# Attention scores four units at a time, the second product over 64 rows in pairs

## The chip, the cores and the metric

The kernel runs on one core of a Trainium2 chip. The core has a matrix engine (TensorE, PE in the profile; its weight loads are the row PEld), three engines for elementwise work (VectorE or DVE, ScalarE or ACT, GpSimd or POOL) and SyncE (SP), whose queue issues most DMA transfers. Matrix products are written to PSUM, eight banks of 128 partitions by 512 floats. The metric is the time of one execution on the device in microseconds; the time before is 445.89 us, the median of three runs (445.73 to 446.54).

## The reference

One encoder layer on a sequence of 1024 tokens with 1024 features. Cut to what matters:

```
h = x @ W_in                                  # q_a,k_a,v_a,z_a, q_b,k_b,v_b,z_b
# group A, 8 heads of 64: 2-D neighbourhood attention on a 16 x 64 grid of tokens
s = q . k over the query's window (8 x 16) / 8 + rel_bias
y_a = softmax(s) @ v
# group B, 8 query heads, 2 key heads: rotary q and k, window |i - j| <= 128, a sink logit
s = q . k / 8, masked;  p = softmax([s, sink])[:-1];  y_b = p @ v
y = concat(y_a * silu(z_a), y_b * silu(z_b)) @ W_out
x = layer_norm(2**0.25 * x + y)
```

All inputs are float32. The kernel works with float16 products and keeps the accuracy by splitting a number into a high and a low half: a product is high x high + high x low + low x high.

## The kernel before, in words

The work has four stages: values (v) for all tokens (TensorE lines L630 and L684, up to about 60 us), six of the 21 other projections of 128 columns each (function `project`, L407), a loop of 128 attention steps (about 122 to 358 us), and the output projection with the layer norm (`out_mms`, L1145, and `final`).

A *unit* is one block of 128 queries of one head. Units 0 to 63 are group B ('b': head pair p, head j of the pair, block of 128 queries i, up to 384 keys); 64 to 127 are group A ('a': a block of 8 x 16 queries, b its column block and `half` its row half, with a window of 11 or 12 grid rows by 24 or 32 columns, 264 to 384 keys). In step i the loop does, among other things:

- `stage_qk` of unit i: two products into one PSUM bank of the tag "s" (L933 and L934), then one VectorE instruction (L943) that adds the bias or mask, takes the minimum and writes the negated scores to one of two tiles `sn`.
- `stage_exp` of unit i: ScalarE (L959) writes the exponentials back into the unit's PSUM bank.
- `stage_tr` of unit i-1: ScalarE (L969) and VectorE (L970) split the exponentials into high and low halves; a DMA transposes them. L970 is the last reader of the bank.
- every fourth step `stage_pv`: the products with the values of a *quad* of four units (L998, bank tag "t"), a step later `stage_on` (L1004, L1007) divides by the sums, and after every second quad `stage_ot` transposes (L1018, tag "t") and multiplies with the gate (L1021 for 'b', L1027 for 'a').
- the other 15 projections and the first part of the output projection as *filling*: `pump_to(u)` issues so many of their products that they are spread evenly over the steps, as the table FILL_AT says.

The queries of a head lie as a stack of 128 rows: for head j = 0 the high half in rows 0 to 63 and the low half in rows 64 to 127, for j = 1 the other way about. The high halves of the keys, `kh`, and the low halves, `kl`, are copied into both halves of the rows (L321 on GpSimd), so a product over 128 rows gives (q_high + q_low) times kh, and the next one (q_high + q_low) times kl:

```python
nc.tensor.matmul(ps[:, :m], q, sl[0], start=True, stop=False)
nc.tensor.matmul(ps[:, :m], q, sl[1], start=False, stop=True)
```

Each engine works off its instructions in the order in which the program writes them. TensorE, VectorE, ScalarE and GpSimd get the filling's evacuations and the splits of weights in between from small queues (`enq`, `pop`), a few per step. PSUM's eight banks are 2 of the tag "pj" (projections), 4 "s" and 2 "t"; a bank is given out again in turn and its next writer waits for its last reader. `m_scale` works out a common scale `zg`, `msc`, `zcol` for the gates in steps 2 to 9, on VectorE.

## Time and profile before

| | |
|---|---|
| median of three runs | 445.89 us |
| the profiled execution | 445.78 us |
| its span, first to last instruction | 444.0 us |
| mean granted TensorE clock | 0.997 |
| TensorE busy (products) | 437.4 us, 99% of the span |
| VectorE / ScalarE / GpSimd busy | 345.6 / 308.2 / 232.2 us |
| score products L933 and L934 | 128 + 128, 4.1% of the chain each |

How to read it: a row of a group gives line, engine, operation, output <- inputs, partitions x elements and type, the count, then busy time in us, the mean in ns of one instruction, and the idle time of the engine just before them with what ended it. A row of the timeline gives the start in us from the beginning of the span, the duration, engine, line, operation and count. Products overlap in the pipe, so the recorded time of one is longer than the distance to the next. The chain of waits is followed back from the last instruction, at each step to what released it.

### The profile page before, as it was taken

What the parts mean: (1) busy time and instruction counts of PE and PEld (TensorE: products, weight loads), DVE (VectorE), ACT (ScalarE), POOL (GpSimd) and SP (SyncE); (2) the same over time, 40 slices, a digit from 0 to 9 for tenths busy, and PEclk for the clock granted to TensorE, in tenths of its full rate; (3) what the DMA queues carried; (4) which work ended last, traced back from release to release, by engine and by line L of the source; (5) the groups of instructions that cost most, each with busy time, mean ns of one, the idle gap of its engine ahead of it and who ended that gap; (6) DMA issues with size and microseconds to landing.
All of it is one profiled execution on the core that took longest, in us unless ns stands there. A gap on an engine that the chain in (4) does not pass through costs nothing.

```text
span 444.0 us, 9533 instructions
## 1 busy us (share of the span) xinstructions
PE 437.4 (99%) x3275; PEld 252.9 (57%) x3275; DVE 345.6 (78%) x861; ACT 308.2 (69%) x717; POOL 232.2 (52%) x242
## 2 busy tenths in 40 slices
PE   9999999999999999999999999999999999999994
PEld 9987754444445565555555656555555654444442
DVE  5999938839989797776898888897767747179954
ACT  7798269866688998798978978797886876002211
POOL 1206834555837658868507638666762455005740
PEclk9999999999999999999999999999999999999998
DMA  8991178976849699687789998999999888101721
GB/s 298 316 362 62 28 249 257 311 264 251 300 98 177 131 190 159 135 149 150 153 165 171 202 173 184 208 180 225 197 201 235 149 198 316 49 0 71 257 76 71
DMA packets 133984, 81.76 MB, mean 184 GB/s; under 512 B 101296, under 2 KB 113328, under 8 KB 133680
## 3 DMA queue, kind: packets, MB, share of 16 engines
q1 hardware_dynamic: 133504, 80.67, 74.4%
q8 instruction: 25, 0.41, 0.4%
q10 hardware_dynamic: 432, 0.49, 0.3%
q14 instruction: 23, 0.19, 0.2%
HBM read 50.73 MB, written 9.96 MB: 137 GB/s over the span
## 4 chain that ended last, share of the span: by engine, by line
PE 92%; DMA 2%; DVE 2%; SPq 1%; ACT 1%; issue 0%; ACTq 0%
PE ps_pj L407 49%; PE ps_s L1145 9%; PE ps_t L998 7%; PE ps_pj L1145 5%; PE ps_t L1145 5%; PE ps_s L933 4%; PE ps_s L934 4%; PE ps_s L684 4%; PE ps_t L1018 2%; PE ps_pj L684 1%; PE ps_t L684 1%; DMA wr<-in_wt 1%; DMA xraw<-in_xT 1%; SPq L625 1%; DVE xm L498 1%; ACT x L455 0%
## 5 line engine op out<-in xcount | busy, mean ns | idle before, releaser
L407 PE MATMUL ps_pj<-xf,wh 128*128 128x512 f16 x672 | 202.6, 379 | 0.0
L407 PE MATMUL ps_pj<-xf,wl 128*128 128x512 f16 x336 | 127.3, 379 | 0.0
L407 PEld LDWEIGHTS <-wh 128*128 128x128 f16 x672 | 63.9, 98 | 60.1 <-issue 0.2
L959 ACT ACTIVATE ps_s<-sn,nm 128x385 f32<-128x385 f32 (+3 forms) x128 | 70.0, 547 | 29.6 <-DVE nm L943 28.6
L970 DVE SCALAR_TENSOR_TENSOR split<-ps_s,split 128x384 f16<-128x384 f32 (+2 forms) x128 | 65.5, 512 | 17.1 <-ACT split L969 16.2
L1145 PEld LDWEIGHTS <-m 128*128 128x128 f16 x408 | 38.8, 98 | 42.7
L969 ACT ACTIVATE split<-ps_s 128x384 f16<-128x384 f32 (+2 forms) x128 | 57.5, 449 | 2.4
L407 PEld LDWEIGHTS <-wl 128*128 128x128 f16 x336 | 32.9, 98 | 36.7
L943 DVE CUSTOM_DVE_ANT_0 sn<-ps_s,bias,sg 128x264 f32<-128x264 f32 (+1 forms) x64 | 35.2, 549 | 15.8 <-PE ps_s L934 6.0
L214 POOL TENSOR_SCALAR wr<-wr,wsc 128x512 f32<-128x512 f32 x26 | 22.0, 847 | 42.5 <-ACT wh L209 36.9
L1145 PE MATMUL ps_s<-wo,m 128*128 128x512 f16 (+1 forms) x192 | 42.0, 372 | 0.0
L943 DVE CUSTOM_DVE_ANT_0 sn<-ps_s,bm,nsk 128x384 f32<-128x384 f32 (+1 forms) x64 | 40.6, 635 | 1.5 <-PE ps_s L934 1.3
L905 POOL TENSOR_SCALAR bias<-bias,rsg 128x552 f32<-128x552 f32 (+1 forms) x24 | 18.6, 775 | 41.7 <-DMA bias<-in_bias 36.9
L933 PE MATMUL ps_s<-ks,qs 128*128 128x384 f16 (+4 forms) x128 | 39.2, 306 | 0.0
L934 PE MATMUL ps_s<-ks,qs 128*128 128x384 f16 (+4 forms) x128 | 39.2, 306 | 0.0
L998 PEld LDWEIGHTS <-tr 128*128 128x128 f16 (+1 forms) x1104 | 36.6, 98 | 2.2
L1202 ACT ACTIVATE sd<-mv,eps 128x1 f32<-128x1 f32 x8 | 2.4, 295 | 44.3 <-DVE mv L1200 42.0
L215 POOL TENSOR_TENSOR wl<-wr,wh 128x512 f16<-128x512 f32 x26 | 31.6, 1214 | 2.2
L1244 POOL TENSOR_TENSOR xr<-xr,gb 128x512 f32<-128x512 f32 x7 | 11.2, 1606 | 39.7 <-ACT xr L1241 39.7
L321 POOL COPY ks<-ks 64x512 f16<-64x512 f16 x40 | 25.9, 660 | 4.7 <-DVE ks L291 1.8
L684 PEld LDWEIGHTS <-xf 128*128 128x128 f16 x216 | 21.0, 98 | 8.3 <-DVE xf L538 0.3
L1145 PE MATMUL ps_pj<-wo,m 128*128 128x512 f16 (+1 forms) x120 | 25.2, 347 | 0.0
(212 smaller groups left out, 820.9 us busy)
## 6 DMA issues: line engine op xcount, KB each, us to landing
ws<-in_wt SPq DMA_DIRECT2D x15, 512.0 KB, 5.6
wr<-in_wt SPq DMA_DIRECT2D x26, 256.0 KB, 3.5
bias<-in_bias SPq DMA_DIRECT2D x16, 276.0 KB, 3.6
wor<-in_wo SPq DMA_DIRECT2D x16, 256.0 KB, 3.7
xr<-in_x SPq DMA_DIRECT2D x8, 512.0 KB, 8.4
xraw<-in_xT SPq DMA_DIRECT2D x15, 256.0 KB, 5.2
out<-xr SPq DMA_DIRECT2D x14, 256.0 KB, 2.0
bias<-in_bias SPq DMA_DIRECT2D x8, 368.0 KB, 3.8
```

Source lines behind the costliest of these rows:

```text
L215: nc.gpsimd.tensor_sub(l, raw, h)
L321: nc.gpsimd.tensor_copy(t[o, sl], t[a, sl])
L407: nc.tensor.matmul(ps, a[:, k % 4, :], mv, start=(k == 0 and i == 0), stop=(k == KT - 1 and i == 2))
L684: nc.tensor.matmul(ps[:, :320], lh[t // 4, k][:, 128 * (t % 4):128 * (t % 4) + 128], rh[k][:, 320 * a:320 * a + 320], start=(k == first an ...
L933: nc.tensor.matmul(ps[:, :m], q, sl[0], start=True, stop=False)
L934: nc.tensor.matmul(ps[:, :m], q, sl[1], start=False, stop=True)
L943: nc.vector.tensor_tensor_reduce(sn[:, :m], ps[:, :m], bias_t, sg[:, c:c + 1], init, op0=ALU.add, op1=ALU.min, accum_out=nm)
L959: nc.scalar.activation(pt[:, :m], sn[:, :m], AF.Exp, bias=nm, scale=-1.0, accum_out=sm[:, k:k + 1])
L969: nc.scalar.activation(hl[:, :m, 0, :c], src, AF.Copy, scale=PSCALE)
L970: nc.vector.scalar_tensor_tensor(hl[:, :m, 1, :c], src, PSCALE, hl[:, :m, 0, :c], op0=ALU.mult, op1=ALU.subtract)
L998: nc.tensor.matmul(ps[:, HD * m:HD * m + HD], a, b_, start=(i == 0), stop=(i == len(mms) - 1))
L1145: nc.tensor.matmul(ps, lh[:, ts], rh[:, cs], start=(e == EO[0] and i == 0), stop=(e == EO[-1] and i == 2))
```

## The change

- The units are put in another order: in 'b' the two heads j of a pair alternate within a block of queries; in 'a' a quad holds the four units (half, j) of one column block in the order (0,0), (1,1), (0,1), (1,0). `slot` keeps the place of a unit in its quad's sums and outputs.
- `stage_qk` is divided. `stage_mm` issues the products of four units at once: four over 128 rows with the high halves of the keys, then four with the low halves that take only the 64 rows with the high queries, `q[a]`; neighbours of these four use different halves of the rows. So q_low times k_low is no longer part of the score. `batch(n)` does this at the end of every fourth step, and `stage_qk` keeps the VectorE part.
- PSUM has 5 banks "s" and one "t". The value products and the transposes of a quad share the one "t" bank, columns 0 to 255 and 256 to 511; other uses of "t" move to "s" or "pj". The third unit of each four writes its exponentials to a tile `px` in SBUF.
- `stage_ot` runs for each quad, three quads after its value products (`OT_AT`), so 'b' gates are multiplied in 16 pieces of 256 columns instead of 8 of 512.
- The filling within four steps is spread by `WARP` instead of evenly, and `QK_AT` says how much of it stands before the batch.
- Part of `m_scale` moves from VectorE to ScalarE, and its steps are set by `M_SCALE`; four scales are kept in `zc` beside the four others.
- The copy of `kl` into the other half of the rows is left out for group A. Bias tiles (`BR`) are six instead of five, loaded by head, and the gate projection "zb3" stands behind "q0".

```diff
-LTT, LPP, BP, BH, BR, ND, NA, NX, F1 = 1, 6, 2, 9, 5, 1, 1, 6, 0.2
+LTT, LPP, BP, BH, BR, ND, NA, NX, F1 = 1, 6, 2, 9, 6, 1, 1, 6, 0.2
-ORDER = ["zb0", "z0", "zb1", "kb", "qb0", "z1", "qb1", "zb2", "qb2", "k0", "qb3", "zb3", "q0", "k1", "q1",
+ORDER = ["zb0", "z0", "zb1", "kb", "qb0", "z1", "qb1", "zb2", "qb2", "k0", "qb3", "q0", "zb3", "k1", "q1",
...
+M_SCALE = (2, 3, 5, 7, 9, 11, 13)
+WARP = (0, 0.33, 0.54, 0.86, 1)
+QK_AT = 0.75
...
-        bufs = {"pj": 2, "s": 4, "t": 2}[tag]
+        bufs = {"pj": 2, "s": 5, "t": 1}[tag]
...
-            dup = [enq("pool", lambda d=dup_: d("kh"), o1, after=32 if dep else 0),
-                   enq("pool", lambda d=dup_: d("kl"), o2, after=36 if dep else 0)]
+            dup = [enq("pool", lambda d=dup_: d("kh"), o1, after=32 if dep else 0)]
+            dup.append(enq("pool", lambda d=dup_: d("kl"), o2, after=36) if dep else o2)
...
             elif i == 4:
-                nc.vector.tensor_scalar_max(zg, zg, 2.0 ** -30)
-                nc.vector.tensor_mul(zg, zg, gm)
+                nc.scalar.mul(zg, zg, gm)
+                nc.scalar.mul(zg, zg, vg)
...
+                nc.scalar.mul(zcol[:, 0:1], vsc, msc)
+                nc.scalar.mul(zcol[:, 1:3], vscb, msc)
...
         for p in range(4):
-            for j in range(2):
-                for i in range(8):
-                    us.append(("b", p, j, i, i % 2 == 1))
+            for i in range(8):
+                for j in range(2):
+                    us.append(("b", p, j, i))
         for p in range(4):
-            for j in range(2):
-                for b in range(4):
-                    for half in range(2):
-                        us.append(("a", p, j, (b, half), half == 1))
+            for b in range(4):
+                for half, j in ((0, 0), (1, 1), (0, 1), (1, 0)):
+                    us.append(("a", p, j, (b, half)))
...
+    def stage_mm(us):
+        for u in us:
+            m, q, sl = qk_parts(u)
+            ps = st[u, "ps"] = bank("s")
+            if units.index(u) == WO_MAX + 4:
+                wo_turn(ps)
+            nc.tensor.matmul(ps[:, :m], q, sl[0], start=True, stop=False)
+        for u in us:
+            m, q, sl = qk_parts(u)
+            a = slice(64 * u[2], 64 * u[2] + 64)
+            nc.tensor.matmul(st[u, "ps"][:, :m], q[a], sl[1][a], start=False, stop=True)
...
-        nc.tensor.matmul(ps[:, :m], q, sl[0], start=True, stop=False)
-        nc.tensor.matmul(ps[:, :m], q, sl[1], start=False, stop=True)
...
-        if g == "b" and t < 2:
+        if g == "b" and t == 0:
             nc.vector.tensor_copy(s0[:, 384:385], nsk[:, h:h + 1])
...
+        if units.index(u) % 4 == 2:
+            pt = ap.tile([128, 388], F32, tag="px", name="px", bufs=1)
...
     def stage_pv(q):
-        ps = st[q, "o"] = bank("t")
+        if q == 0:
+            st["t"] = bank("t")
+        ps = st["t"]
...
     def pump_to(u):
         n = 0
+        k = int(u) % 4
+        u = int(u) // 4 * 4 + 4 * (WARP[k] + (WARP[k + 1] - WARP[k]) * (u - int(u)))
...
+    OT_AT = {(q, 0): (q - 3,) for q in range(3, 30)}
+    OT_AT.update({(30, 0): (27,), (31, 0): (28,), (31, 2): (29,), (32, 0): (30, 31)})
...
-            stage_qk(u)
+            if i == 0:
+                batch(0)
+            stage_qk(units[i])
...
         if i < NU:
             stage_exp(units[i])
+        if i % 4 == 3 and i + 1 < NU:
+            pump_to(i + QK_AT)
+            batch(i + 1)
```

How the instructions stand, at two places. In these rows the first word is the line, then the operation, the output <- inputs with buffer numbers, and the output's size. The first place is TensorE in the 'b' half, before: a unit's two score products (tiles `qs`, queries, and `ks`, keys) between the filling's products (`wh`, `wl`, weights; `xf`, tokens).

```order
L407 LDWEIGHTS wl19_2058
L407 MATMUL ps_pj_2393<-xf14_518,wl19_2058 128x512
L933 LDWEIGHTS qs_2293
L933 MATMUL ps_s_2451<-ks_1339,qs_2293 128x256
L934 LDWEIGHTS qs_2293
L934 MATMUL ps_s_2451<-ks_1350,qs_2293 128x256
L407 LDWEIGHTS wh19_2057
L407 MATMUL ps_pj_2393<-xf16_519,wh19_2057 128x512
```

TensorE at the same place of the changed kernel: the last two products over 128 rows of a batch of four units, and then its four over 64 rows.

```order
L934 LDWEIGHTS qs_2283
L934 MATMUL ps_s_2443<-ks_1339,qs_2283 128x384
L934 LDWEIGHTS qs_2285
L934 MATMUL ps_s_2445<-ks_1339,qs_2285 128x384
L938 LDWEIGHTS qs_2283
L938 MATMUL ps_s_2439<-ks_1350,qs_2283 128x256
L938 LDWEIGHTS qs_2285
L938 MATMUL ps_s_2441<-ks_1350,qs_2285 128x256
L938 LDWEIGHTS qs_2283
L938 MATMUL ps_s_2443<-ks_1350,qs_2283 128x384
L938 LDWEIGHTS qs_2285
L938 MATMUL ps_s_2445<-ks_1350,qs_2285 128x384
```

What moved: the second products no longer follow the first ones of their unit, and they alternate between the query stacks of the two heads (2283 and 2285). The second place is VectorE in steps 5 to 7 before (L943 appears as ISA, its second row reads the minimum out; L970 is the split; `zg` is the gates' scale).

```order
L970 SCALAR_TENSOR_TENSOR split_1137<-ps_s,split_1137 128x3x128
L797 TENSOR_TENSOR zg<-zg,wg 128x1 x2
L338 STREAM_SHUFFLE rp_sw<-rp_raw 128x512
L943 ISA sn_1139,nm<-ps_s,bm,nsk,sg 128x384
L943 ISA nm 128x1
L970 SCALAR_TENSOR_TENSOR split_1138<-ps_s,split_1138 128x3x128
L799 TENSOR_SCALAR zg<-zg 128x1
L800 TENSOR_TENSOR zg<-zg,gm 128x1
```

The same stretch of VectorE in the changed kernel:

```order
L991 SCALAR_TENSOR_TENSOR split_1137<-ps_s,split_1137 128x3x128
L799 TENSOR_REDUCE zg<-zc 128x1
L342 STREAM_SHUFFLE rp_sw<-rp_raw 128x512
L963 ISA sn_1139,nm<-ps_s,bm,nsk,sg 128x384
L963 ISA nm 128x1
L991 SCALAR_TENSOR_TENSOR split_1138<-ps_s,split_1138 128x3x128
```

What moved: the products of the scale (L800 before) have left VectorE, and its maxima over four weights (L797) are one reduction.

More of the change, by code (lines that the diff above doesn't have):

```diff
@@ L686, in v16 @@
                              start=(k == first and i == 0), stop=(k == KT - 1 and i == 2))
-        set_a = [bank(r) for r in ("s", "pj", "t", "s")]
+        set_a = [bank(r) for r in ("t", "pj", "s", "s")]
         for i in range(3):
@@ L896, in stage_load @@
             b, half = t
-            if half == 0 and b != 2:
+            key = p, j, b - (b == 2)
+            if st.get(("bias", j), (None,))[0] != key:
                 bulk["last"] = clock["step"] + 1
@@ L976, in quad @@
     def quad(q):
[L977 to L978 removed]
+        g, p, j, t = units[4 * q]
+        return g, p, t // 2 if g == "b" else t[0]
     def stage_pv(q):
[L981 removed]
+        if q == 0:
+            st["t"] = bank("t")
+        ps = st["t"]
         for m in range(4):
             u = units[4 * q + m]
[L984 removed]
+            g, p, j, t = u
             n, ch = geom(u)
@@ new lines, in stage_ot @@
+    def stage_ot(*qs):
+        ps = st["t"]
+        for n, q in enumerate(qs):
+            g, p, h = quad(q)
+            need(*stk_ops.get(f"zb{p}" if g == "b" else f"z{p}", ()))
+            o = on.pop(q).rearrange("p m e -> p (m e)")
+            c = 256 * (n if len(qs) > 1 else 1)
+            for i in range(2):
+                nc.tensor.transpose(ps[:, c + 128 * i:c + 128 * i + 128], o[:, 128 * i:128 * i + 128], identf)
+        for n, q in enumerate(qs):
+            g, p, h = quad(q)
+            c = 256 * (n if len(qs) > 1 else 1)
+            if g == "b":
+                z = zt[4 + p][:, 256 * h:256 * h + 256]
+                nc.vector.scalar_tensor_tensor(z, ps[:, c:c + 256], z_col(4 + p), z, op0=ALU.mult, op1=ALU.mult)
+            else:
+                z = zt[p].rearrange("p (r c) -> p r c", c=GW)[:, :, 16 * h:16 * h + 16]
+                src = ps[:, c:c + 256].rearrange("p (r c) -> p r c", c=16)
@@ L1290, in gain_load, with batch @@
         nc.sync.dma_start(gain_tile[0], gain.partition_broadcast(128))
+    def batch(n):
+        us = units[n:n + 4]
+        for u in us:
+            if u[3] in (0, 4):
+                need(*stk_ops[f"b{u[1]}", u[2], u[3] // 4])
+            if u[0] == "a" and n % 16 == 0:
+                need(*stk_ops[u[1], u[2], 0], *stk_ops[u[1], u[2], 1])
+        stage_mm(us)
+    OT_AT = {(q, 0): (q - 3,) for q in range(3, 30)}
+    OT_AT.update({(30, 0): (27,), (31, 0): (28,), (31, 2): (29,), (32, 0): (30, 31)})
     clock["step"] = 0
```

139 lines of the change are left out of this document (57 added, 82 removed).

## The prediction

> **What bounds the kernel now.** I read the first part of the page, then busy time by stretches of the span, then the chain of waits summed by line.
>
> ```profile
> PE 437.4 (99%) x3275; PEld 252.9 (57%) x3275; DVE 345.6 (78%) x861; ACT 308.2 (69%) x717; POOL 232.2 (52%) x242
> 120.00:160.00 40.00, 40.00 (x317) 21.86 (x316) 34.53 (x106) 33.23 (x84) 25.10 (x24) 1.00 0.71 138
> 280.00:320.00 40.00, 40.00 (x364) 23.35 (x363) 34.07 (x93) 33.88 (x87) 27.87 (x35) 1.00 1.04 198
> by line: PE ps_pj L407 49.0%; PE ps_s L1145 9.0%; PE ps_t L998 7.3%; PE ps_pj L1145 5.0%; PE ps_t L1145 4.7%; PE ps_s L933 4.1%; PE ps_s L934 4.1%; PE ps_s L684 3.7%; PE ps_t L1018 1.6%; PE ps_pj L684 1.5%; PE ps_t L684 1.5%; DMA wr<-in_wt
> ```
>
> In the stretch rows the columns after the sum are PE, PEld, DVE, ACT and POOL. In the attention steps TensorE is busy all the time at full clock (1.00), VectorE 85 to 86% and ScalarE 83 to 85%. The chain is TensorE lines almost alone. Busy time could hide short waits, since a product's recorded duration overlaps its neighbour's, so I looked at starts in the timeline:
>
> ```profile
> 199.78 0.33 PE L933 MATMUL ps_s<-ks,qs 128*128 128x384 f16 x1
> 199.94 0.33 PE L934 MATMUL ps_s<-ks,qs 128*128 128x384 f16 x1
> 200.10 0.59 PE L407 MATMUL ps_pj<-xf,wh 128*128 128x512 f16 x2
> 200.53 0.38 PE L407 MATMUL ps_pj<-xf,wl 128*128 128x512 f16 x1
> ```
>
> A product of 384 columns is followed 0.16 us later by the next, one of 512 after 0.215 us. These are the rates of the streamed columns (0.42 ns each) and nothing lies between. So the kernel is bound by the sum of TensorE's products; what leaves TensorE leaves the span, if nobody else becomes late. The profiled execution took 445.78 us (444.0 in the span, 1.8 around it), 0.1 below the median of the runs; the sum starts from 445.8.
>
> **The change, part by part.**
>
> *The second products over 64 rows.* L934 multiplies the stacked queries (high part in one half of the rows, low part in the other) by the low part of the keys over 128 rows. The new L938 takes only the high queries, 64 rows, in the upper half of the array for one head and the lower half for the other. The new unit order puts the two heads next to each other, so that two such products can run side by side. The chain gives L934 4.1% of 444.0, or 18.2 us, for 64 x 384 + 16 x (256 + 264 + 288 + 352) = 43,136 columns, again 0.42 ns each. If a pair takes as long as its wider member: in the 'b' half members are equal, 22,528 columns become 11,264; in the 'a' half a pair joins 11 with 12 grid rows, and each batch keeps two times 12 rows of the window: 24 x (24 + 32 + 32 + 24) x 4 = 10,752. Together 22,016 columns, 9.3 us. Saved: 8.9 us. All of it is on the bounding engine.
>
> *Changing from 128 rows to 64 and back.* This happens twice a batch, 64 times. No product of before uses half the rows, so the price must be bounded. The nearest rows at the low end are those where the kind of product changes:
>
> ```profile
> 253.56 0.29 PE L934 MATMUL ps_s<-ks,qs 128*128 128x288 f16 x1
> 253.68 0.60 PE L1018 MATMUL ps_t<-identf,on 128*128 128x128 f32 x4
> 254.12 1.22 PE L998 MATMUL ps_t<-va,tr 96*128 96x64 f16 x36
> 255.17 0.59 PE L407 MATMUL ps_pj<-xf,wh 128*128 128x512 f16 x2
> L933 PE MATMUL ps_s<-ks,qs 128*128 128x384 f16 x64 | 20.9, 326 | 0.0
> L934 PEld LDWEIGHTS <-qs 128*128 128x128 f16 x128 | 12.5, 98 | 15.1
> ```
>
> From 128 rows of f16 to four f32 transposes, to 36 products over 96 rows (1.05 us, 29 ns each), and back to 128 rows: no gap at any of the three places. So 0 is the low end (a gain excluded, since nothing but the pairing is left to save). The high end comes from the last two rows: a product lasts 326 ns where its columns take 162, so its tail is 164 ns; if the array must be empty before the rows are regrouped, and the next weights (98 ns) may only be loaded then, a change costs up to 262 ns. I take half the tail, 82 ns: the tail row is nearer in kind than the 96-row one, which still uses the whole height, but the tail also holds the way of the results to memory, and regrouping only needs the array empty. 64 x 82 ns is 5.2 us. At the ends the sum of the changes is 0, 10.5 (the tail alone) or 16.8 us. The change pays up to (8.9 - 0.8) / 64 = 127 ns, with the 0.8 us of the next item.
>
> A rule of the Trainium skill speaks to this: the page "TensorEngine Tiling (Array Packing)", Key Properties, says that changing the tiling mode, and not just the tile, drains the TensorE. No product in the trace of before shows such a change; the rule gives no time, and by it the sum would lie nearer to the tail's 10.5 us than to the 0 of the 96-row products.
>
> *Four scores at once, five banks.* Before, a unit's bank was needed again by the unit four later, once its split (L970) had read it. Now batch k+1's third product needs the bank of unit 4k+1 (after its split), the fourth that of unit 4k+2 (after L943 only, since every third unit of a batch writes its exponentials to a tile px). The batch sits just before the place where the old score of unit 4k+4 stood. Its third product would start there + 0.32 - 0.20 us (two products later, 0.8 of a filling product earlier by the new spreading):
>
> ```profile
> 134.92 0.27 PE L933 MATMUL ps_s<-ks,qs 128*128 128x256 f16 x1
> 135.24 0.55 DVE L970 SCALAR_TENSOR_TENSOR split<-ps_s,split 128x384 f16<-128x384 f32 x1
> 208.73 0.27 PE L933 MATMUL ps_s<-ks,qs 128*128 128x256 f16 x1
> 209.09 0.55 DVE L970 SCALAR_TENSOR_TENSOR split<-ps_s,split 128x384 f16<-128x384 f32 x1
> 287.21 0.45 DVE L970 SCALAR_TENSOR_TENSOR split<-ps_s,split 128x288 f16<-128x288 f32 x1
> 289.32 0.31 PE L933 MATMUL ps_s<-ks,qs 128*128 128x352 f16 x1
> ```
>
> Unit 5's bank comes free at 135.79, and the third product of the batch that starts with unit 8 would want it at 135.04: 0.75 us late. Unit 45's comes free at 209.64 against 208.85: 0.8 late. In the 'a' half it is early, unit 89's at 287.66 against 289.44. So TensorE can be held up in the first half only, between 0 and, with a few smaller ones beside the two, some 2.6 us.
>
> *Gate scale on ScalarE.* It stands on VectorE in just those early steps:
>
> ```profile
> 132.17 0.36 DVE L797 TENSOR_TENSOR zg<-zg,wg 128x1 f32<-128x1 f32 x2
> 133.77 0.34 DVE L797 TENSOR_TENSOR zg<-zg,wg 128x1 f32<-128x1 f32 x2
> 135.89 0.30 DVE L800 TENSOR_TENSOR zg<-zg,gm 128x1 f32<-128x1 f32 x1
> 137.10 0.32 DVE L802 TENSOR_TENSOR zg<-zg,vg 128x1 f32<-128x1 f32 x1
> L938 DVE COPY sn<-nsk 128x1 f32<-128x1 f32 x16 | 2.3, 144 | 0.0
> L1202 ACT ACTIVATE sd<-mv,eps 128x1 f32<-128x1 f32 x8 | 2.4, 295 | 44.3 <-DVE mv L1200 42.0 <-DVE rstd L1207 2.1
> L1027 DVE SCALAR_TENSOR_TENSOR z<-ps_t,zcol,z 128x256 f32<-128x256 f32 x16 | 7.0, 477 | 7.6 <-PE ps_t L1018 7.6
> L1021 DVE SCALAR_TENSOR_TENSOR z<-ps_t,zcol,z 128x512 f32<-128x512 f32 x8 | 6.0, 746 | 0.0
> L321 POOL COPY ks<-ks 64x512 f16<-64x512 f16 x40 | 25.9, 660 | 4.7 <-DVE ks L291 1.8 <-DVE ks L289 0.8 <-ACT ks L283 0.5
> ```
>
> The four rows are 1.3 us that VectorE loses by step 9, and eight of the copies of a sink column (144 ns) go too. Four small ScalarE operations come, at most 295 ns each, 1.2 us, in a stage where ScalarE has 15% idle. That covers unit 5's 0.75 us but not unit 45's; I book one wait of 0.8 us. (What is queued behind a waiting score product is all of TensorE's filling, so it counts in full.)
>
> *The rest, at nothing.* The 'b' gate products, 8 of 512 columns, become 16 of 256: 16 x 477 - 8 x 746 ns = 1.7 us more VectorE over 64 steps with 15% idle; uncovered it would be a part of the 2.6 us. Sixteen copies of low keys leave POOL (660 ns each, 10.6 us), which is busy for only 52% of the span. One bank for value products (columns 0 to 255) and transposes (256 to 511) instead of two: the next use is four steps later, about 7 us, and the reader's work is under 1 us. Bias loads keep number and size and now come two in a row, seven steps ahead; SP's list has as many rows as before. The fourth 'b' gate after the first 'a' queries is the same products in another order, and its users come later too (step 69). Outside the steps the same products stand in other banks.
>
> Sum: 445.8 - 8.9 + 5.2 + 0.8 = 442.9 us.
>
> **The rivals.**
>
> *Changes cost the whole tail or more (slower).* The drain empties the array and the pipe behind it. For it: no row shows that weights or columns can pass a regrouping; against it: every change of kind in the trace is free. With 164 ns it gives 445.8 - 8.9 + 10.5 + 0.8 = 448.2 us, with the weight load behind it 454.5. It decides from 127 ns on. The page named above is the rule behind this one.
>
> *Changes are free.* The 96-row products speak for it; against it, they never leave the full height. 445.8 - 8.9 + 0.8 = 437.7 us.
>
> *The pairs do not run side by side*, so that the change doesn't do what it says. A product's time is its columns, whatever its rows: the 96-row products with 64 columns keep the 29 ns of full ones. Then nothing is saved: 445.8 + 5.2 + 0.8 = 451.8 us. Against this rival stands the Trainium skill, page "TensorE: Matmul & The Clock Gate", Part 3, The mechanism, which has products in different row groups start about 4 ns apart; no run here shows it yet.
>
> *The banks hold TensorE up (slower).* VectorE now gets its first score of four only after the batch: 0.97 us after its start instead of 0.33, some 0.65 later. If nothing relieves the 2.6 us, and ten of the first half's batches are late by another 0.65 each, that is 2.6 + 6.5 = 9.1 in place of 0.8: 445.8 - 8.9 + 5.2 + 9.1 = 451.2 us. It decides from 3.7 us of waiting on. Against it: each wait moves TensorE back against VectorE once, and the next batch finds the bank free.
>
> **How the numbers follow.** The forecast as worked out, with 30 to 110 ns a change, gives 439.6 to 444.7 us: chance 0.50. Free changes 0.12, the whole tail or more 0.22, no pairing 0.04, banks 0.06, and 0.06 for a price near the 127 ns at which it comes out even. Changes of 0.2% (0.9 us) are about what a measurement of this kernel can tell from none. So faster 0.62, same 0.06, slower 0.32. The likeliest case's own range is 439.6 to 444.7; the one for 8 in 10 takes in the nearer half of the free case and the tail alone: 438.0 to 449.0.
>
> **What would show it.** Right: in each batch the four 64-row products start in two pairs, the members a few ns apart, and the four take some 0.32 us for 384 columns; before the first and after the last stands a gap of about 0.08 us; TensorE's other starts are as now; VectorE waits for scores once in four units. Wrong: starts 0.16 us apart inside the 64-row part (no pairing), gaps above 0.13 us (slower), or gaps ahead of the third and fourth 128-row product of batches in the first 50 steps (banks).

## The result, and the profile after

The changed kernel takes 448.12 us (median of four runs, 447.75 to 448.48). The kernel before took 446.04 in the four runs beside it. The ratio is 1.0043 with a 95% interval of 1.0031 to 1.0055: slower by about 2 us, where 3 us less were forecast. The profiled execution took 448.48 us with a span of 446.7, against 445.78 and 444.0 before.

From the page of the kernel after, busy time and the engines' shares of the chain; then the stretches of 40 us in the same columns as before:

```profile
PE 437.7 (98%) x3275; PEld 241.9 (54%) x3275; DVE 348.1 (78%) x851; ACT 310.9 (70%) x721; POOL 225.6 (51%) x226
...
PE 69%; issue 9%; DVE 9%; ACT 6%; POOL 5%; DMA 1%; POOLq 0%; DVEq 0%; ACTq 0%
```

```profile
120.00:160.00 40.00, 38.89 (x286) 18.47 (x284) 33.98 (x91) 32.97 (x85) 25.12 (x23) 1.00 0.69 144
280.00:320.00 40.00, 40.00 (x362) 21.39 (x361) 34.95 (x93) 34.58 (x85) 25.78 (x30) 1.00 1.11 203
```

TensorE is no longer busy all the time in the early steps: 38.89 of 40 us instead of 40.00. In the later steps it is as full as before. Its share of the chain fell from 92 to 69%, and VectorE, ScalarE and GpSimd, which were hardly in it, now have 20% together. That is no measure of the time lost: once a wait has led the chain to another engine, it can stay there while TensorE goes on working, and TensorE's busy share fell by one point only. TensorE still sets the time nearly everywhere, but now it is waiting for others in places.

**One batch, from the timeline.** Four products over 128 rows, four over 64, and the next projection products, with the loads of their weights:

```profile
253.30 0.62 PEld L934 LDWEIGHTS <-qs 128*128 128x128 f16 x4
253.51 0.79 PE L934 MATMUL ps_s<-ks,qs 128*128 128x352 f16 x4
254.23 0.11 PEld L938 LDWEIGHTS <-qs 64*128 64x128 f16 x4 [0.30 <-issue]
254.23 0.49 PE L938 MATMUL ps_s<-ks,qs 64*128 64x352 f16 x4
254.65 0.11 PEld L411 LDWEIGHTS <-wh 128*128 128x128 f16 x2 [0.30 <-issue]
254.65 0.60 PE L411 MATMUL ps_pj<-xf,wh 128*128 128x512 f16 x2
```

The first four have 352, 384, 352 and 384 columns, 0.62 us at 0.42 ns each; the first product over 64 rows starts 0.72 us after the first of them. So 0.10 us lies between. Two pairs whose wider members have 384 columns would need 0.32 us; the next projection product starts 0.42 us later. Again 0.10 us. The single records give 96 to 97 ns for each of the 64 changes, both ways. Inside the 64-row part of this batch the pairs start 0.16 us apart. The two members of a pair start 3 to 4 ns apart in 48 of the 64 pairs and 13 to 17 ns apart in the other 16, the second pairs of the 'a' half. The pairing works as forecast and saves 9.0 us; the changes cost 6.2.

The weight loads show the form of the price. Loads of an unchanged row count run ahead of the products that use them, here by 0.21 us (253.30 against 253.51); the first load after a change starts together with its product, after 0.30 us without a load that nothing in the profile explains:

```profile
L938 PEld LDWEIGHTS <-qs 64*128 64x128 f16 x128 | 3.6, 94 | 10.7 <-issue 10.7
```

**The banks.** The timeline around the third batch ("b" half), VectorE and TensorE only:

```profile
135.07 0.49 PE L934 MATMUL ps_s<-ks,qs 128*128 128x384 f16 x2
135.62 0.08 DVE L963 DVE_READ_ACCUMULATOR2_ANT nm<- 128x1 f32 x1
135.62 0.55 DVE L991 SCALAR_TENSOR_TENSOR split<-ps_s,split 128x384 f16<-128x384 f32 x1
135.75 0.79 PE L934 MATMUL ps_s<-ks,qs 128*128 128x384 f16 x2 [0.19 <-DVE nm L963]
```

The third product could start at 135.40 (two products of 0.16 us after 135.07) and starts at 135.75, right behind L963 of the earlier px unit. The fourth needs the bank that the split L991 frees at 136.17, and starts at 136.22. Such waits stand in five batches, at 135, 142, 149, 202 and 210 us, and sum to 2.43 us by the single records. There is none in the second half.

**The transposes.** Two stand behind the value products now, where four stood after every second quad:

```profile
257.44 0.42 PE L1040 MATMUL ps_t<-identf,on 128*128 128x128 f32 x2
257.69 0.38 PE L411 MATMUL ps_pj<-xf,wl 128*128 128x512 f16 x1
```

0.25 us for two, against 0.44 for four before (253.68 to 254.12 in the rows of before). In the single records the second transpose follows the first after 143 ns here and after 109 ns before; the next product follows the last transpose after 109 ns in both. So a pair behind value products costs 34 ns more, once, and 29 pairs stand like that: 1.0 us. A pair that stands behind an ordinary product, at 371.81 us, takes 0.22 us, with no such extra.

**The end of the loop.** The last transposes and what follows them on TensorE and VectorE:

```profile
372.77 0.65 PE L1040 MATMUL ps_t<-identf,on 128*128 128x128 f32 x4
373.46 0.88 DVE L1050 SCALAR_TENSOR_TENSOR z<-ps_t,zcol,z 128x256 f32<-128x256 f32 x2 [0.75 <-PE ps_t L1040]
374.40 1.90 PE L1170 MATMUL ps_t<-wo,m 128*128 128x512 f16 x8 [0.97 <-DVE eps L1191]
```

The transposes are done with at 373.21 (four by 0.11 us) and TensorE's next product, into the same bank "t", starts at 374.40, when both gate products have read it. That is 1.2 us of nothing; with 0.1 us that these transposes wait for the gate product of the quad before them, in the same bank, it is the 1.3 us of the table below. The profile names a VectorE memset (eps) as the releaser, which only stands behind the gate products in the same queue. Before, the answering rows had no gap, since there were two banks "t":

```profile
368.71 0.60 PE L1018 MATMUL ps_t<-identf,on 128*128 128x128 f32 x4
369.15 1.03 PE L1145 MATMUL ps_t<-wo,m 128*128 128x512 f16 x4
```

Set against the profiled execution of before, all in us:

| term | forecast | measured |
|---|---|---|
| pairs side by side | -8.9 | -9.0 |
| 64 changes of the row count | +5.2 | +6.2 |
| waits for banks "s" | +0.8 | +2.4 |
| transposes two by two | 0 | +1.0 |
| last transposes and the one bank "t" | 0 | +1.3 |
| start of the first projection, 59.44 to 59.98 us | 0 | +0.5 |
| sum | -2.9 | +2.4 |

The two profiled executions differ by 2.7 us, so 0.3 are not placed. The start of the projections scatters: among kernels whose code up to there is the changed kernel's it stood between 58.99 and 60.18 us. Half a microsecond between two single executions can be that alone.

### The profile page after: what moved, and what is told of

The parts are those of the page before. It is cut to its first block, busy times and chain, and to the rows that moved or that the text cites. A ratio compares the mean times of both kernels' runs of the same rounds, so it can differ in the third digit from the quotient of the medians.

```text
span 446.7 us, 9468 instructions
## 1 busy us (share of the span) xinstructions
PE 437.7 (98%) x3275; PEld 241.9 (54%) x3275; DVE 348.1 (78%) x851; ACT 310.9 (70%) x721; POOL 225.6 (51%) x226
## 4 chain that ended last, share of the span: by engine, by line
PE 69%; issue 9%; DVE 9%; ACT 6%; POOL 5%; DMA 1%; POOLq 0%; DVEq 0%; ACTq 0%
PE ps_pj L411 26%; PE ps_s L1170 11%; PE ps_t L1022 6%; PE ps_pj L1170 5%; PE ps_s L688 4%; PE ps_s L634 4%; PE ps_s L934 3%; POOL wl L217 2%; PE ps_t L1170 2%; PE ps_s L938 2%; ACT ps_s L980 2%; PE ps_pj L634 2%; PE ps_t L1040 2%; POOL wr L216 2%; DVE sn L963 2%
## 5 line engine op out<-in xcount | busy, mean ns | idle before, releaser
L411 PEld LDWEIGHTS <-wh 128*128 128x128 f16 x672 | 64.9, 98 | 72.6 <-issue 2.7
L980 ACT ACTIVATE ps_s<-sn,nm 128x385 f32<-128x385 f32 (+3 forms) x96 | 52.4, 546 | 19.9 <-DVE nm L963 18.7
L991 DVE SCALAR_TENSOR_TENSOR split<-ps_s,split 128x384 f16<-128x384 f32 (+2 forms) x96 | 49.1, 511 | 12.6 <-ACT split L990 12.2
L1170 PE MATMUL ps_s<-wo,m 128*128 128x512 f16 (+1 forms) x240 | 53.5, 374 | 0.0
L990 ACT ACTIVATE split<-ps_s 128x384 f16<-128x384 f32 (+2 forms) x96 | 43.3, 451 | 2.0
L963 DVE CUSTOM_DVE_ANT_0 sn<-ps_s,bm,nsk 128x384 f32<-128x384 f32 (+1 forms) x64 | 40.6, 635 | 0.2
L963 DVE CUSTOM_DVE_ANT_0 sn<-ps_s,bias,sg 128x264 f32<-128x264 f32 (+1 forms) x64 | 35.0, 547 | 2.6 <-PE ps_s L938 1.9
L934 PE MATMUL ps_s<-ks,qs 128*128 128x384 f16 (+4 forms) x128 | 24.6, 306 | 1.3 <-DVE split L991 0.8
L991 DVE SCALAR_TENSOR_TENSOR split<-px,split 128x384 f16<-128x384 f32 (+2 forms) x32 | 23.2, 724 | 3.3 <-ACT split L990 3.2
L688 PE MATMUL ps_s<-wf,xf 128*128 128x320 f16 x144 | 23.8, 299 | 0.0
```

The source lines that it names most:

```text
L411: nc.tensor.matmul(ps, a[:, k % 4, :], mv, start=(k == 0 and i == 0), stop=(k == KT - 1 and i == 2))
L688: nc.tensor.matmul(ps[:, :320], lh[t // 4, k][:, 128 * (t % 4):128 * (t % 4) + 128], rh[k][:, 320 * a:320 * a + 320], start=(k == first an ...
L963: nc.vector.tensor_tensor_reduce(sn[:, :m], ps[:, :m], bias_t, sg[:, c:c + 1], init, op0=ALU.add, op1=ALU.min, accum_out=nm)
L980: nc.scalar.activation(pt[:, :m], sn[:, :m], AF.Exp, bias=nm, scale=-1.0, accum_out=sm[:, k:k + 1])
L990: nc.scalar.activation(hl[:, :m, 0, :c], src, AF.Copy, scale=PSCALE)
L991: nc.vector.scalar_tensor_tensor(hl[:, :m, 1, :c], src, PSCALE, hl[:, :m, 0, :c], op0=ALU.mult, op1=ALU.subtract)
```

## The experiments

Each kernel is the changed one with the edit shown, and was timed beside the kernel before (446.2 to 446.3 us there).

**1. The second products over all 128 rows.**

```diff
-            a = slice(64 * u[2], 64 * u[2] + 64)
-            nc.tensor.matmul(st[u, "ps"][:, :m], q[a], sl[1][a], start=False, stop=True)
+            nc.tensor.matmul(st[u, "ps"][:, :m], q, sl[1], start=False, stop=True)
```

with the copy of the low keys made for group A again.

> The changed kernel with the four second products of a batch over 128 rows again (both halves of the queries, low keys copied into both halves of the rows); batches, banks and order stay. My reading of the trace after: side by side the pairs save 9.0 us of TensorE, and 64 changes between 128 and 64 rows cost 6.2 us (96 ns each). Then this kernel is 2.8 us slower than the changed one: about 450.9 us, with no gap of about 0.1 us before and after the second products. Rival (the changes of row count cost more than the pairing saves): it is faster than the changed one, below 447 us.

449.94 us (449.75 to 450.12), ratio 1.0079 (1.0062 to 1.0096). A batch in its timeline:

```profile
253.96 0.79 PE L934 MATMUL ps_s<-ks,qs 128*128 128x352 f16 x4
254.59 0.79 PE L937 MATMUL ps_s<-ks,qs 128*128 128x352 f16 x4
255.21 0.59 PE L411 MATMUL ps_pj<-xf,wh 128*128 128x512 f16 x2
```

0.63 and 0.62 us for four products, and no gap at either border. So the 0.10 us belong to the change of rows and to nothing else in the batch. Taking the 64-row products away makes the kernel 1.8 us slower than the changed one. By the terms it would be 9.0 - 6.2 = 2.8 us, less 0.7 for the bank waits, which are 1.75 us here instead of 2.43: 2.1. So the pairing pays for its changes, and the rest of the change loses more than it wins.

**2. Batches of two units.** Twice as many changes, and less to ask of the banks at once.

```diff
-        us = units[n:n + 4]
+        us = units[n:n + 2]
...
-        if i % 4 == 3 and i + 1 < NU:
+        if i % 2 == 1 and i + 1 < NU:
```

> The changed kernel with batches of two units instead of four: two products over 128 rows, then one pair over 64. There are 128 changes of row count instead of 64, and no product waits for a bank, since five banks hold two batches. By 96 ns a change: 6.2 us more, less the 2.4 us of bank waits: about 451.9 us. Rival (the bank waits are all that matters, a change costs nothing by itself): 445.7 us.

452.77 us (452.09 to 453.25), ratio 1.014 (1.0125 to 1.0155). The gap ahead of the 64-row products is again 96 ns, now 64 times, and behind them 97 ns, 61 times among the projection products; no wait between 128-row products is left. Relative to the changed kernel these two are +6.0 and -2.4 us, and the measured difference is 4.65. The price of a change is confirmed as a fixed one; about 1 us of the difference is not placed. The bank waits can thus be removed, but twice as many changes cost more than that gives.

**3. A second tile px.** The second and third unit of each four write their exponentials to SBUF, so that the bank of unit 4k+1 comes free earlier.

```diff
-        if units.index(u) % 4 == 2:
-            pt = ap.tile([128, 388], F32, tag="px", name="px", bufs=1)
+        if units.index(u) % 4 in (1, 2):
+            pt = ap.tile([128, 388], F32, tag="px", name="px", bufs=2)
```

with five split tiles instead of six, for the room.

> The changed kernel with the second and the third unit of each four writing their exponentials to SBUF (two px tiles), so a batch needs no bank that waits for a split; to make room there are five tiles of split halves instead of six. If the 2.4 us between the 128-row products of batches 2, 3, 4, 11 and 12 are waits for the bank of a batch's second unit, they go: about 445.9 us. Rival (VectorE and ScalarE are simply too slow there, and the wait moves to the next product or the next batch): 447.5 us or more.

450.68 us (450.37 to 452.0), ratio 1.01 (1.0082 to 1.0119): worse. The waits did not go, they grew to 3.97 us. From its chief waits of TensorE, and its groups of the split:

```profile
PE ps_s L934 <- DVE nm L963: 2.3, 4, 1.0
```

```profile
L991 DVE SCALAR_TENSOR_TENSOR split<-px,split 128x384 f16<-128x384 f32 x40 | 31.4, 786 | 7.1 <-ACT split L990 6.9
...
L991 DVE SCALAR_TENSOR_TENSOR split<-ps_s,split 128x384 f16<-128x384 f32 x40 | 22.1, 552 | 7.2 <-ACT split L990 6.8
```

The fourth product now waits for L963, the next reader in VectorE's order, so the rival held. In front of the two latest of these L963, at 149.52 and 210.91 us, stand splits from PSUM and steps of other work (L372, L1046, L293), no split from px. The five split tiles are not the reason either: ScalarE waits 2.7 us for one of them to be read out, but in four places from 248 us on, where no score product waits for a bank. What the rows above do show is a price of px: a split that reads it takes 786 ns, one that reads PSUM 552. The changed kernel has the same difference in its own groups:

```profile
L991 DVE SCALAR_TENSOR_TENSOR split<-ps_s,split 128x384 f16<-128x384 f32 x60 | 33.2, 553 | 9.2 <-ACT split L990 8.8
L991 DVE SCALAR_TENSOR_TENSOR split<-px,split 128x384 f16<-128x384 f32 x20 | 15.3, 766 | 2.6 <-ACT split L990 2.5
```

With the narrower forms (629 against 452 ns eight times, 702 against 421 four times) px costs VectorE 4.3 + 1.4 + 1.1 = 6.8 us that the forecast had at nothing. Where it comes from is seen in the single rows (below, in the section on the hardware).

**4. Another bank for the last transposes.**

```diff
-        ps = st["t"]
+        ps = st["t"] if len(qs) == 1 else bank("s")
...
-        for t, tag in ((0, "s"), (1, "s"), (2, "t")):
+        for t, tag in ((0, "t"), (1, "s"), (2, "s")):
```

> The changed kernel with the last transposes (quads 30 and 31) in a bank of the tag s, and the free t bank for the first output product that follows. If the about 1.2 us that TensorE stands still after them is the wait for their reader on VectorE to leave the one t bank, it goes: about 446.9 us. Rival (the output products wait for the gates themselves, or for the reuse of memory by the last stage): no change, 448.1 us.

446.59 us (446.25 to 447.63, ten runs), ratio 1.0011 (1.0002 to 1.002). The end of its loop:

```profile
366.80 0.60 PE L1040 MATMUL ps_s<-identf,on 128*128 128x128 f32 x4
367.24 2.75 PE L1170 MATMUL ps_s<-wo,m 128*128 128x512 f16 x12
```

No gap is left, and the 1.5 us that the kernel gains are most of what the change had lost. Expected and found. The later experiments 7 to 12 start from this kernel.

**5. The four gate-scale products of steps 9 and 13 on VectorE again.**

```diff
-                nc.scalar.mul(zg, zg, gm)
-                nc.scalar.mul(zg, zg, vg)
+                nc.vector.tensor_mul(zg, zg, gm)
+                nc.vector.tensor_mul(zg, zg, vg)
...
-                nc.scalar.mul(zcol[:, 0:1], vsc, msc)
-                nc.scalar.mul(zcol[:, 1:3], vscb, msc)
+                nc.vector.tensor_mul(zcol[:, 0:1], vsc, msc)
+                for i in range(2):
+                    nc.vector.tensor_mul(zcol[:, 1 + i:2 + i], vscb[:, i:i + 1], msc)
```

> The changed kernel with the gate scale's four products (steps 9 and 13) back on VectorE. If these early steps are held up by VectorE's load, four operations of about 0.3 us make the waits of batches 3 and 4 longer by up to 1.2 us: 448.3 to 449.3 us. Rival (the place of the scale doesn't matter there): 448.1 us.

451.42 us (450.42 to 451.56), ratio 1.011 (1.0094 to 1.0126): 3.3 us slower than the changed kernel, more than expected. The bank waits rise from 2.4 to 4.5 us, in the batches at 142.5 and 150.4. Its timeline there, GpSimd and VectorE:

```profile
141.29 1.18 POOL L217 TENSOR_TENSOR wl<-wr,wh 128x512 f16<-128x512 f32 x1
...
141.48 1.00 DVE L804 TENSOR_TENSOR zg<-zg,vg 128x1 f32<-128x1 f32 x1
...
149.78 1.30 DVE L810 TENSOR_TENSOR zcol<-vscb,msc 128x1 f32<-128x1 f32 x2
149.80 1.27 POOL L345 TENSOR_TENSOR rp_raw<-rp_raw,rp_sw 128x512 f32<-128x512 f32 x1
```

A product of one element per partition takes 1.00 us, and ends where GpSimd's instruction ends (142.48 against 142.47). So this move is worth more than its few instructions: 2.1 us through the banks, and 1.2 us whose place was not found.

**6. The px units' low half on GpSimd.** Two instructions there instead of L991 for every fourth unit.

```diff
+        if units.index(u) % 4 == 2:
+            nc.gpsimd.tensor_scalar(src, src, psc, 1.0, op0=ALU.mult, op1=ALU.mult)
+            nc.gpsimd.tensor_sub(hl[:, :m, 1, :c], src, hl[:, :m, 0, :c])
+        else:
```

> The changed kernel with the low half of each third unit's exponentials, the ones in the SBUF tile px, made by GpSimd (a scaling and a subtraction) instead of VectorE. In the trace after, VectorE's split from px takes 766 ns for 384 columns against 553 from PSUM; it lasts until a GpSimd operation that was under way ends and some 0.42 us more, and takes its usual 0.55 us where GpSimd is idle. My theory now: VectorE, burdened by these, comes late to the banks of batches 2, 3, 4, 11 and 12. Then VectorE loses 23 us and the bank waits of 2.4 us fall below 0.8: about 446.4 us. Rival (VectorE's load is not what makes the banks late, or GpSimd, which gets some 46 us more, delays the weights' low halves): 448 us or more.

452.29 us (451.81 to 456.36), ratio 1.0165 (1.011 to 1.022): a miss, and the rival held. From its waits:

```profile
POOL px L994 <- ACT split L992: 30.6, 13, 7.5
```

GpSimd, which works in order, now stands 30.6 us waiting for ScalarE's halves, what is queued behind comes later, and the bank waits of TensorE are 6.5 us. A quarter of VectorE's splits less did not help, since the engine that took them was needed for something else.

**7. The transposes ahead of the value products**, on the kernel of experiment 4, so that they would stand behind ordinary products.

```diff
-        if m == 0 and 0 <= q < NU // 4:
-            stage_pv(q)
         if (q, m) in OT_AT:
             stage_ot(*OT_AT.pop((q, m)))
+        if m == 0 and 0 <= q < NU // 4:
+            stage_pv(q)
```

> The changed kernel with the last transposes in a bank of the tag s, as before in e5_tail_bank (446.6 us), and each quad's two transposes ahead of the value products instead of behind them. Behind the short value products (29 ns apart) two transposes take 0.25 us to the next product; in the kernel before, four behind a score took 0.44. If the 15 ns each come from their weight loads (about 140 ns) standing open behind short products, 32 times 0.03 us go: about 445.6 us. Rival (the extra time belongs to two transposes instead of four): 446.6 us.

468.89 us (468.7 to 469.58), ratio 1.0509 (1.0493 to 1.0526): a miss by 23 us. Its timeline:

```profile
256.65 0.38 PE L1040 MATMUL ps_t<-identf,on 128*128 128x128 f32 x2
257.07 0.48 DVE L1046 SCALAR_TENSOR_TENSOR z<-ps_t,zcol,z 128x256 f32<-128x256 f32 x1 [0.61 <-PE ps_t L1040]
257.61 1.03 PE L1022 MATMUL ps_t<-vb,tr 128*128 128x64 f16 x30 [0.57 <-DVE z L1046]
```

The value products write other columns of the one bank "t", and still wait until the gate product has read the transposes: 0.83 us by the single records, 29 times, 24 us. This is the wait of the tail, laid into every quad. In the changed kernel only the order hides it. The question itself is answered by the single records: behind ordinary products the second transpose follows the first after 109 to 110 ns in every pair, so the 34 ns do come from the value products ahead, and not from there being two transposes instead of four. The loading of the first transpose's weights starts only 28 ns ahead of it behind the value products (at 257.4 us in the changed kernel), and 214 ns ahead of it here (at 256.6 us).

**8. Experiments 6 and 7 in one kernel**, with the edits of both.

> The three edits together: low halves of the px units on GpSimd, transposes ahead of value products, the last transposes in a bank of the tag s. If the reasons given for the single ones hold and add: 448.1 - 1.7 - 1.0 - 1.5, about 443.9 us, which would be 0.5% below the kernel before. If the bank waits are not VectorE's load: 445.6 us or more.

471.73 us (471.2 to 472.3), ratio 1.057 (1.0553 to 1.0587). 2.8 us above experiment 7, where the edit of experiment 6 by itself had cost 4.2: the two faults add up in part.

**9 and 10. The batch later on TensorE.** The kernel of experiment 4 with

```diff
-QK_AT = 0.75
+QK_AT = 1.25
```

and, in the second kernel, 1.6.

> The kernel with the last transposes in a score bank (446.6 us), and each batch of scores put half a step later on TensorE: QK_AT from 0.75 to 1.25, so that about half a step of projection work (a step is about 1.8 us) stands ahead of the batch instead of behind it. Theory: the waits between the 128-row products (2.4 us in five batches) come from banks that VectorE gives back up to 0.63 us too late; with the batch some 0.9 us later nearly all are gone, and VectorE, which is a unit ahead of what it needs, loses nothing: 446.6 - 1.8 to 2.4 = 444.2 to 444.8 us, below the kernel before. Rival: VectorE takes up the new scores as soon as they stand, so its whole chain moves by the same 0.9 us, the next banks come that much later, and the waits come back: 446.3 to 447.5 us with waits of 1.5 us or more between the products, or ahead of the value products, whose transposed halves then come later.

> The same with QK_AT 1.6, a further third of a step. Theory: no wait between the 128-row products is left, 444.0 to 444.8 us, no more than 0.3 us from the kernel with 1.25. Rival: VectorE and ScalarE run out of scores, since a batch is 1.5 us later than before for every four units, and the value products or the next batch wait for them: over 447 us, and slower than with 1.25.

448.46 us (447.96 to 449.0), ratio 1.0058 (1.0044 to 1.0072), with 1.25; 447.39 (447.07 to 448.18), ratio 1.0032 (1.0021 to 1.0044), with 1.6. Both are slower than 446.59, so the theory fell. The waits at 135, 194 and 202 us are gone as it said, but those at 142 and 149 us grew: 3.02 us in sum with 1.25 and 2.01 with 1.6. What grew is seen in the timeline of the first of them, ScalarE, VectorE and TensorE at the batch of 149.6 us:

```profile
148.11 0.62 ACT L289 CAST qs<-rp_raw 64x512 f16<-64x512 f32 x1 [1.11 <-POOL rp_raw L345]
...
149.15 0.56 DVE L991 SCALAR_TENSOR_TENSOR split<-ps_s,split 128x384 f16<-128x384 f32 x1 [1.67 <-ACT split L990]
...
150.33 0.54 DVE L963 CUSTOM_DVE_ANT_0 sn<-ps_s,bm,nsk 128x256 f32<-128x256 f32 x1
...
150.93 0.32 PE L934 MATMUL ps_s<-ks,qs 128*128 128x384 f16 x1 [0.90 <-DVE nm L963]
```

Filling that is issued earlier brings its own evacuations earlier: the cast of a query, which waits 1.1 us for GpSimd, now stands ahead of ScalarE's half of the split, VectorE waits 1.67 us for that half, and TensorE in the end for VectorE. In the kernel of experiment 4 the same cast came behind the halves of this batch:

```profile
148.59 0.49 ACT L990 ACTIVATE split<-ps_s 128x384 f16<-128x384 f32 x1
150.11 0.62 ACT L289 CAST qs<-rp_raw 64x512 f16<-64x512 f32 x1 [0.54 <-POOL rp_raw L345]
```

The later batch also leaves a wait for a gate in the output projection near 352 us, of 0.8 us with 1.25 and 1.1 us with 1.6. Neither theory nor rival had named this: not the score came late, the order of ScalarE's queue had changed.

**11. The gate scale one step later**, on the kernel of experiment 4.

```diff
-M_SCALE = (2, 3, 5, 7, 9, 11, 13)
+M_SCALE = (2, 3, 6, 7, 10, 12, 14)
```

> The kernel with the last transposes in a score bank (446.6 us), and the gate scale one step later: M_SCALE (2, 3, 6, 7, 10, 12, 14) for (2, 3, 5, 7, 9, 11, 13). In steps 9 and 13 its ScalarE products stand between the score of unit 4k+1 and its exponentials and split, whose bank the next batch's third product wants; in steps 10 and 14 they stand behind that split. Theory: a product lasts 0.29 us and the next starts 0.19 after it, so the split comes 0.36 us earlier in each place: the waits at the batches of 142 and 149 us (0.47 and 0.62) fall to about 0.1 and 0.3, the other three stay: 446.6 - 0.7 = 445.9 us. Rival: ScalarE runs in order behind other work (the gate piece L371, the query cast L289 that waits for GpSimd), so the time is only taken up by these, or VectorE comes late for another unit: waits within 0.2 us of 2.4 in sum, and 446.3 to 446.9 us.

(The product that waits there is the batch's fourth, not its third.) 447.34 us (447.04 to 448.15), ratio 1.0031 (1.0021 to 1.004): 445.9 was expected. At the place itself it went as expected. The timeline of the batch at 142 us in the kernel of experiment 4 and in this one:

```profile
141.65 0.60 PE L934 MATMUL ps_s<-ks,qs 128*128 128x384 f16 x3
142.55 0.27 PE L934 MATMUL ps_s<-ks,qs 128*128 128x256 f16 x1 [0.30 <-DVE split L991]
```

```profile
142.04 0.84 PE L934 MATMUL ps_s<-ks,qs 128*128 128x384 f16 x4
142.81 0.45 PE L938 MATMUL ps_s<-ks,qs 64*128 64x384 f16 x4
```

The wait there falls from 0.47 to 0.14 us and that at 149 us from 0.62 to 0.44. But the batch at 194 us now waits 0.28 instead of 0.02, others by small amounts, and the sum goes only from 2.40 to 2.14 us. The spans of the two profiled executions are 444.7 and 444.9. Why the timed runs are 0.7 us longer is not known.

**12. The fourth 'b' gate ahead of the first 'a' queries again**, on the kernel of experiment 4: this part of the change undone.

```diff
-"qb3", "q0", "zb3", "k1"
+"qb3", "zb3", "q0", "k1"
...
-ZSUM = (1, 6, 13, 14)
+ZSUM = (1, 5, 13, 14)
```

> The kernel with the last transposes in a score bank (446.6 us), and the fourth 'b' gate before the first 'a' queries again, as in the kernel before (its sum back at place 5). Theory: these are the same products in another order; their readers come at step 69 and 57, both late; within 0.4 us of 446.6, with the waits of the batches at 194 to 209 us (0.02 + 0.10 + 0.47) moved by at most 0.4, since the gate's ScalarE and VectorE pieces and the queries' casts change places there. Rival: the order sets which of ScalarE's and GpSimd's work stands ahead of those splits: the waits of the late 'b' batches change by 1 us or more, or the first 'a' batch waits for its queries: 447.6 us or more.

449.27 us (448.94 to 451.05), ratio 1.0078 (1.0063 to 1.0094), 2.7 us slower than experiment 4; the rival held. Its timeline at the last 'b' batch:

```profile
210.26 0.69 DVE L372 SCALAR_TENSOR_TENSOR z<-z,ps_pj 128x512 f32<-128x512 f32 x1 [1.60 <-ACT z L371]
210.87 0.54 DVE L963 CUSTOM_DVE_ANT_0 sn<-ps_s,bm,nsk 128x256 f32<-128x256 f32 x1
...
211.47 0.32 PE L934 MATMUL ps_s<-ks,qs 128*128 128x384 f16 x1 [1.45 <-DVE nm L963]
```

VectorE stands 1.6 us before the second step of a gate piece (L372), the score behind it (L963) is late, and the bank with it: 1.6 us at this product where experiment 4 had 0.16. All bank waits are 3.9 us. So the order of gate and queries, booked at nothing, is worth 2.7 us, 1.5 of them as bank waits; the other 1.2 were not placed.

## Why the prediction was wrong

The sign was wrong. The range of 438.0 to 449.0 us held the time, near its upper end. The sum of the terms went from -2.9 to +2.4 us, by 5.3: 1.0 for the price of the changes, 1.6 for the bank waits, 2.8 for what stood under "the rest, at nothing", and 0.1 the other way for the pairing. That the rival of the whole tail gives 448.2 us, the measured time, is chance: its price of 164 ns was not found.

- *The pairing* was right in kind and size: members 3 to 4 ns apart in three pairs of four, -9.0 us against -8.9. That rule of the Trainium skill which spoke for it (page "TensorE: Matmul & The Clock Gate", Part 3, The mechanism, about 4 ns) agrees with the trace.
- *The change of the row count* was right in kind, a gap at each border, which agrees with the drain of which the Trainium skill's page "TensorEngine Tiling (Array Packing)", Key Properties, speaks; the size was half the tail, 82 ns, and 96 to 97 were measured, +1.0 us in sum. It stayed under the 127 ns at which it comes out even, and experiment 1 shows the pairing as a gain. The rivals of the whole tail (164 ns), of no price, and of no pairing fell.
- *The bank waits* were found in the right batches and kind, and mis-sized: one wait of 0.8 us was booked, five batches with 2.4 us came. The step that failed in it is "That covers unit 5's 0.75 us". VectorE does lose the four products, but the batch of unit 5 itself, at 135 us, still waits 0.67 us. In the batches at 142 and 149 us, what ScalarE got stands ahead of its halves of the splits that the banks wait for, and VectorE stands still for these halves, 0.22 and 0.34 us:

```profile
142.62 0.56 DVE L991 SCALAR_TENSOR_TENSOR split<-ps_s,split 128x384 f16<-128x384 f32 x1 [0.22 <-ACT split L990]
148.35 0.29 ACT L809 ACTIVATE zcol<-vscb,msc 128x2 f32<-128x2 f32 x1
149.28 0.49 ACT L990 ACTIVATE split<-ps_s 128x384 f16<-128x384 f32 x1
149.80 0.56 DVE L991 SCALAR_TENSOR_TENSOR split<-ps_s,split 128x384 f16<-128x384 f32 x1 [0.34 <-ACT split L990]
```

These splits read PSUM and take their usual 0.56 us. The 6.8 us that px adds to VectorE lie in other splits, and how they bear on the waits is not shown. The product that waits for the split is mostly the fourth of its batch, and not the third as the prediction had it. The rival "banks" was the right mechanism at a quarter of its 9.1 us, below the 3.7 at which it would have decided.
- *"The rest, at nothing"* is the step that turned the sign. With the two sizes above put right the sum would still be 445.8 - 9.0 + 6.2 + 2.4 = 445.4 us, no difference to speak of. Then come 1.3 us for the one bank "t" in the tail, 1.0 for the transposes by twos, and the 0.5 us at the start, which can be scatter. The argument on the bank (four steps between two uses) holds for the loop, where experiment 7 shows how much it hides; it was not asked what follows the last transposes, when no steps are left. Experiment 4 confirms that term by itself: with another bank there the kernel is 1.5 us faster and differs from the one before by 0.1%. The transposes were costed by their VectorE readers only; that their own time depends on what stands ahead of them was not looked at.
- *The gate scale and the order of the gate* were put at nothing or at a small gain. Undone by themselves they cost 3.3 and 2.7 us. So the change contains the cure for part of the trouble that its batches bring.

What stays open: the 2.4 us of bank waits could be moved or made a little smaller (experiments 3, 6, 9 to 11), and were removed only at the price of 64 more changes (experiment 2), so it is not shown that a kernel without them would take the 444.2 us that experiment 4 less 2.4 us gives; how much of them is owed to px was not isolated, since no kernel without px was run; why weights that are loaded late behind value products delay the second transpose and not the first; and the 0.3 us of the sum that have no place.

## What to carry to other kernels

When buffers are shared out anew, look at the last use in the program as well as at the loop: a bank whose reader is hidden for 30 rounds can stand open in the final one. Moving the work that caused a wait of half a microsecond did not remove the waiting in experiments 3, 6 and 9 to 11, because in-order queues handed it on to the next reader; cost such a change by the order of every queue it passes, and not by the duration of what moves. And when a result is moved from PSUM to SBUF to free a bank, price its readers again: they may now meet another engine.

## What the runs showed of the hardware

A change between products over 128 rows and over 64 rows costs 96 to 97 ns, either way, whether 64 or 125 of them were made, and the first weights after it are not loaded ahead.

A VectorE instruction with both inputs in SBUF waits for the GpSimd instruction that is under way; one with an input in PSUM does not. From the changed kernel's timeline:

```profile
136.51 1.27 POOL L344 TENSOR_TENSOR rp_sw<-rp_sw,sin 128x512 f32<-128x512 f32 x1
...
137.03 1.16 DVE L991 SCALAR_TENSOR_TENSOR split<-px,split 128x384 f16<-128x384 f32 x1 [0.27 <-ACT split L990]
```

GpSimd's instruction ends at 137.78, the split at 138.19, 0.41 us later. So it is each time: of the 20 splits of 384 columns that read px, 12 start under an instruction of GpSimd and end 0.40 to 0.42 us after it, and the other eight take 0.55 to 0.56 us. Of the 60 splits of that size that read PSUM, 43 start under an instruction of GpSimd, and all of them take 0.54 to 0.56 us. The one-element products of experiment 5 show the same without any length of their own. This agrees with the Trainium skill, page "SBUF — State Buffer", section Who interferes with whom: a VectorE instruction with two SBUF inputs contends with a GpSimd instruction that reads SBUF, and the later one blocks. That rule spoke against px, and the prediction did not weigh it.
